# RWKV stage of a two-layer trunk: a list scheduler that also models the DMA queue and the staging buffers, and a norm over two row tiles

## The chip, the core and the metric

The kernel runs on one core of one Trainium2 chip. The metric is the device time of one execution in microseconds (us), as the median of three runs. The engines are named as the profile names them: PE is TensorE (PEld its weight loads), DVE is VectorE, ACT is ScalarE, POOL is GpSimd, and SP is SyncE, which here issues nearly all DMAs, in the order of its program. Each engine works through its own program in order; an instruction whose inputs are not there holds up everything behind it on that engine.

## What is computed

The input is 512 rows of 1024 channels. Layer 0 is an RWKV-7 time mixing, layer 1 a differential attention; each is followed by a layer norm over a scaled residual and a squared-ReLU MLP with another such norm. Everything is float32. Cut to what the change touches, layer 0 is

```
xx = token_shift(x) - x
r, k, v = (x + xx*mu[0]) @ w_r, (x + xx*mu[2]) @ w_k, (x + xx*mu[3]) @ w_v
w = -softplus(-(w0 + tanh(xw @ w1) @ w2)) - 0.5
a = sigmoid(a0 + (xa @ a1) @ a2);   g = sigmoid(xg @ g1) @ g2
kk = k*k_k / norm(k*k_k);   k = k * (1 + (a - 1) * k_a)
# per head of 64 channels, over the 512 rows:
S_t = S_{t-1} diag(exp(-exp(w_t))) + (S_{t-1} a_t) b_t^T + v_t k_t^T,  a_t = -kk, b_t = kk*a
y_t = S_t r_t
y = layer_norm(y per head) + sum(r*k*r_k) * v
h = (y * g) @ w_o
x = layer_norm(ALPHA*x + h)           # the norm that the change pairs
```

## The kernel before

Matrix products of the float32 data are made as three products of high and low parts (`mm3`, L138 to L143), so each weight is loaded, cast to a high part by ACT and subtracted to a low part by POOL or DVE.

The RWKV stage (`rwkv`, L172) works on eight pairs of heads (128 channels), p = 0 to 7, in four groups g of two pairs. The recurrence is cut in eight chunks of 64 rows. Its work consists of small generators, each a step with a letter and a number:

- `K`, `L`, `H`, `M`: the low-rank parts and the mixed inputs.
- `u0` to `u23`: a weight unit of `w_k`, `w_r`, `w_v` (L293): two loads of 256 KB into the staging tile `wst` (three buffers), two casts to `whi` on ACT (L307), two subtractions to `wlo` on POOL (L310). `p0` to `p11`: the projections, four of k, four of r, four of v, 48 matmuls each (L315). `E`: evictions, which store k, r and v to DRAM (L348). `D`, `N`: the norms of k.
- `F`, the front of a pair (`front`, L574): loads `wa`, k, r and the norms (L581 to L588), four matmuls (L593, L594), a chain over ACT, DVE (L602, L620 to L624) and POOL (L91), then the bonus: a matmul (L640), a load of v (L645), a product on DVE (L649), a store to `bD` (L652).
- `A` (`amat`, L654): 16 matmuls (L671), four masked evictions on DVE (L676), a store to `nbD` (L679). `B` (`tmat`, L683): transposes (L697).
- `I` (`inverse`, L704), one for a group of two pairs: a load of `nu` from `nbD` (L714), 15 steps of two small DVE operations each (L724, L726), a store to `gbD` (L727). `J` (`inverse2`, L730): a load of `dc` from `gbD` (L738), then the rest of the inverse in a chain of PE, DVE and ACT, whose first matmul is L752.
- `U`, `X`, `S`, `Y`, `Z`: the solve, the values, the scan over the chunks (L868 to L883), the head norm, and the finish (L915), which loads `g2` (L919) and `bl`, the stored bonus (L921). `P`: preparation of `w_o` (two staging buffers, loads L391, ACT L396, POOL L400); `P0` also loads x into `acc` (L384, two loads of 1 MB). `W`, `V`: the output projection of a group and its addition to `acc`.

What stands in which order on the engines is decided while the program is built, by `order` (L515): a list scheduler that takes, of all steps whose needs are met, the one that can start first by its own count of the engines' time, and of those within `SLACK` the one with the longest path behind it (`SPAN`, a planned length for each letter). A yield names an engine and a planned duration. A yield `"SP"` is a plain delay: SP is not counted as an engine, so a DMA is issued wherever the plan stands at that moment, and the staging buffers are not counted.

The last group, `W(3)`, and the layer norm of each 128-row tile (`ln`, L986) are written after the list and ordered by the framework's own scheduler. `ln` takes one row tile: two BN_STATS (L992), an aggregate, a reciprocal root in ten small DVE operations (`rsqrt`, L93 to L103), an affine half on DVE (L1002, L1003), a normalised half on ACT (L1008), transposes on PE (L1022), then splits. The MLP's first matmuls come behind the four tiles' transposes.

## Time and profile before

| what | us |
|---|---|
| median of the runs | 1543.22 (1542.98 to 1543.57) |
| the profiled execution | 1538.03 |
| its span, first to last instruction | 1536.1 |
| PE busy in the span | 1393.3 (91%) |
| DVE, ACT, POOL busy | 732.4, 589.7, 324.7 |

The profiled execution is 5.2 us shorter than the median. The share of busy time is over the whole span; the RWKV stage, with the norm behind it, is about its first 539 us, and the idle time of PE lies mostly there. In the rows below a timeline row gives start, length, engine, line, operation and tiles, and in brackets the idle time just ahead of it with what ended it. "SPq" is SP issuing a DMA. [...]

### The profile page before, as it was taken

The page shows a single profiled execution, that of the slowest core. Times are in us where ns is not written, and L with a number is a line of the kernel's source. Part 1 is how long each engine was busy: PE and PEld are TensorE (multiplying, and loading weights), DVE is VectorE, ACT ScalarE, POOL GpSimd, SP SyncE. Part 2 cuts the span into 40 slices and gives each one's busy share as a digit, 9 for nine tenths or more (in the row PEclk, how much of TensorE's full clock was granted, in tenths as well). Part 3 has the DMA queues.
Part 4 walks back from the last instruction along what each step waited for, and adds up shares of the span by engine and source line. Part 5 has one row for each costly group of instructions (what it writes and reads, how often), then busy time and mean ns, then how long its engine had stood idle before and what let it go on. Part 6 is the DMA issues. An engine that isn't in the chain of part 4 may idle for free.

```text
span 1536.1 us, 25128 instructions
## 1 busy us (share of the span) xinstructions
PE 1393.3 (91%) x10200; PEld 1148.3 (75%) x10200; DVE 732.4 (48%) x1558; ACT 589.7 (38%) x1091; POOL 324.7 (21%) x252
## 2 busy tenths in 40 slices
PE   8999939689995499999999989999988999999997
PEld 3677718467783398888888878888877988888886
DVE  6210465668747723333333553456667433333346
ACT  7422434355243332332313244566554513233220
POOL 5344420311013220010101044223232201010010
PEclk9999959789997699999999999999988999999999
DMA  4234534332304213232323035223212433233311
GB/s 162 90 122 144 159 79 112 108 100 84 96 27 153 68 55 111 84 108 90 102 96 96 28 102 159 74 79 110 63 62 77 138 96 96 96 96 97 96 42 55
DMA packets 81155, 146.31 MB, mean 95 GB/s; under 512 B 32224, under 2 KB 36992, under 8 KB 81040
## 3 DMA queue, kind: packets, MB, share of 16 engines
q1 hardware_dynamic: 81040, 144.71, 30.6%
q8 instruction: 80, 1.31, 0.4%
q14 instruction: 35, 0.29, 0.1%
HBM read 127.30 MB, written 13.19 MB: 91 GB/s over the span
## 4 chain that ended last, share of the span: by engine, by line
PE 75%; DVE 13%; issue 4%; DMA 3%; SPq 2%; ACT 2%; POOL 1%; DVEq 0%; POOLq 0%; ACTq 0%
PE a L141 11%; PE a L142 11%; PE a L143 10%; PE o L142 5%; PE s L143 5%; PE o L143 5%; PE s L142 5%; PE s L141 5%; PE o L141 5%; PE o L1204 1%; PE e L259 1%; DMA wst<-in_wo 1%; PE e L260 1%; DVE gtm L724 1%; DVE gu L726 1%
## 5 line engine op out<-in xcount | busy, mean ns | idle before, releaser
L106 ACT CAST whi<-wst 128x1024 fp32r<-128x1024 f32 x160 | 168.0, 1053 | 314.7 <-PE a L143 124.5
L107 DVE TENSOR_TENSOR wlo<-wst,whi 128x1024 fp32r<-128x1024 f32 x120 | 147.5, 1230 | 234.0 <-ACT whi L106 234.0
L91 POOL TENSOR_TENSOR r<-r 128x512 f32<-128x512 f32 x64 | 67.6, 1056 | 536.3 <-ACT hh L1063 534.7
L141 PE MATMUL a<-ba,whi 128*128 128x512 f32 (+1 forms) x400 | 147.9, 370 | 2.6 <-DVE qT L1152 2.2
L142 PE MATMUL a<-ba,whi 128*128 128x512 f32 (+1 forms) x400 | 146.3, 366 | 0.0
L143 PE MATMUL a<-ba,wlo 128*128 128x512 f32 (+1 forms) x400 | 146.2, 365 | 0.0
L107 POOL TENSOR_TENSOR wlo<-wst,whi 128x1024 fp32r<-128x1024 f32 x40 | 96.1, 2417 | 168.3 <-ACT whi L106 167.9
L1065 DVE TENSOR_TENSOR hl<-r,hh 128x512 fp32r<-128x512 f32 x64 | 44.3, 692 | 146.5 <-POOL r L91 146.5
L141 PEld LDWEIGHTS a<-ba,whi 128*128 128x128 f32 x400 | 76.0, 190 | 18.1 <-issue 3.7
L143 PEld LDWEIGHTS a<-ba,wlo 128*128 128x128 f32 x400 | 76.0, 190 | 12.0
L142 PEld LDWEIGHTS a<-ba,whi 128*128 128x128 f32 x400 | 76.1, 190 | 11.4
L141 PE MATMUL s<-ba,whi 128*128 128x512 f32 (+1 forms) x232 | 81.9, 353 | 0.0
L143 PE MATMUL s<-ba,wlo 128*128 128x512 f32 (+1 forms) x232 | 81.6, 352 | 0.0
L142 PE MATMUL s<-ba,whi 128*128 128x512 f32 (+1 forms) x232 | 81.3, 351 | 0.0
L310 POOL TENSOR_TENSOR wlo<-wst,whi 128x512 fp32r<-128x512 f32 x48 | 61.8, 1304 | 86.8 <-ACT whi L307 86.8
L142 PE MATMUL o<-ba,whi 128*128 128x512 f32 (+1 forms) x200 | 71.8, 359 | 3.6 <-DVE ba L107 3.6
L141 PE MATMUL o<-ba,whi 128*128 128x512 f32 (+1 forms) x200 | 71.8, 359 | 1.3 <-ACT ba L106 1.3
L143 PE MATMUL o<-ba,wlo 128*128 128x512 f32 (+1 forms) x200 | 71.6, 358 | 0.0
L141 PE MATMUL o<-whi,hh 128*128 128x512 f32 x176 | 68.7, 390 | 0.0
L142 PE MATMUL o<-wlo,hh 128*128 128x512 f32 x176 | 68.6, 390 | 0.0
L143 PE MATMUL o<-whi,hl 128*128 128x512 f32 x176 | 68.3, 390 | 0.0
L142 PE MATMUL a<-wlo,hh 128*128 128x512 f32 x168 | 65.4, 390 | 0.0
(287 smaller groups left out, 3316.4 us busy)
## 6 DMA issues: line engine op xcount, KB each, us to landing
wst<-in_m SPq DMA_DIRECT2D x128, 512.0 KB, 3.7
wst<-in_kv SPq DMA_DIRECT2D x16, 512.0 KB, 3.9
wst<-in_wk SPq DMA_DIRECT2D x16, 256.0 KB, 7.2
wst<-in_wr SPq DMA_DIRECT2D x16, 256.0 KB, 4.1
wst<-in_wv SPq DMA_DIRECT2D x16, 256.0 KB, 3.3
wst<-in_wo SPq DMA_DIRECT2D x16, 256.0 KB, 7.1
wst<-in_q SPq DMA_DIRECT2D x8, 512.0 KB
kT<-kT SPq DMA_DIRECT2D x16, 256.0 KB, 2.9
```

What stands on the lines that cost most here:

```text
L91: return eng.tensor_tensor(out=out, in0=in0, in1=in1, op=ALU.mult)
L106: self.nc.scalar.copy(out=hi, in_=src)
L107: (lo_eng or self.nc.vector).tensor_tensor(out=lo, in0=src, in1=hi, op=ALU.subtract)
L141: mm(ps, lh, rh, start=first, stop=False)
L142: mm(ps, lh, rl, start=False, stop=False)
L143: mm(ps, ll, rh, start=False, stop=last)
L259: PE.matmul(ps, lx[:, c, c0:c0 + P], x0(c), start=(c == 0), stop=False)
L260: PE.matmul(ps, ls[:, c, c0:c0 + P], xs(c), start=False, stop=(c == NK - 1))
L310: G.tensor_tensor(out=lo[:, b:b + 2], in0=ss[b // 2], in1=hi[:, b:b + 2], op=ALU.subtract)
L724: V.tensor_tensor(out=tmv, in0=GU[:, 0:m, s:s + 1].to_broadcast([P, m, n]), in1=NU[:, s:s + 1, s + 1:16].to_broadcast([P, m, n]), op=ALU.mult)
L726: V.tensor_tensor(out=gv, in0=gv, in1=tmv, op=ALU.add)
L1065: V.tensor_tensor(out=hl, in0=r, in1=hh, op=ALU.subtract)
```

## The change

- `order` gets an engine `Q`, the DMA queue, free from 8.0 on, which is occupied in turn by every yield `"Q"`; loads and stores now stand behind such yields. The plain delay `"SP"` remains for the time to landing.
- It also counts the staging buffers: `ws` (3, of the projection weights) and `wo` (2, of `w_o`). Units `u` and `P` are cut in halves, each with its own load, cast and subtraction.
- The steps `F`, `A`, `B` of all pairs and `I0`, `I1` get 250 added to their rank, so they are taken first where they can start at about the same time as another step.
- The front's second part loads v ahead of its bonus matmul. The loads of `g2` and `bl` become a step of their own, `T`, ahead of `Z`. `P3` no longer waits for `W2` but for `P2`. Several planned durations are altered.
- `ln` takes a list of row tiles; behind `W(3)` it is called twice with two tiles (`last`), with one reciprocal root of two columns. The other norms call it with one tile.

The core of the diff:

```diff
 SLACK = 0.3
+EARLY = 250
@@ unit
                 for b in range(0, h, 2):
+                    yield "Q", 1.6, 1, "ws"
                     ss.append(self.t(self.ws, "wst", [P, 2, WCOL]))
                     nc.sync.dma_start(...)
-                yield "SP", 4.5
-                yield "ACT", 1.24
+                yield "SP", 2.2
                 for b in range(0, h, 2):
+                    yield "ACT", 0.62
                     S.copy(out=hi[:, b:b + 2], in_=ss[b // 2])
-                yield "POOL", 2.7
                 for b in range(0, h, 2):
+                    yield "POOL", 1.3
                     G.tensor_tensor(out=lo[:, b:b + 2], ...)
+                    self.drop(1, "ws")
@@ W(3)
+            def last(w):
+                ...
+                next(w)
+                for b in range(0, NT, 2):
+                    for _ in range(4):
+                        next(w, None)
+                    for i in range(2 * b, 2 * b + 4):
+                        self.add_out(el["w3"][i], i // 2, i % 2, 1.0)
+                    self.ln(0, gb, (b, b + 1), False)
@@ needs
-                need["Z%d" % p] = ["Y%d" % g, "F%d" % p] + (old("Z", 1) if q else []) + (["W%d" % (g - 1)] if g else [])
+                need["T%d" % p] = ["o1", "F%d" % p] + old("Z", 1)
+                need["Z%d" % p] = ["Y%d" % g, "T%d" % p] + (["W%d" % (g - 1)] if g else [])
-                need["P%d" % g] += ["S4", "S5"] if g == 3 else []
+                if g == 3:
+                    need["P3"] = ["S4", "S5", "P2"]
@@ order
         free = self.free = dict.fromkeys(("PE", "DVE", "ACT", "POOL", "SP"), 0.0)
+        free["Q"] = 8.0
-        self.left = {"e": 4, "in": 5, "cs": 1}
+        self.left = {"e": 4, "in": 5, "cs": 1, "ws": 3, "wo": 2}
+        early = ["%s%d" % (t, p) for t in "FAB" for p in range(8)] + ["I0", "I1"]
                 rank[n] = SPAN[n[0]] + max([path(m) for m in after[n]], default=0.0)
+                rank[n] += EARLY * (n in early)
@@ ln
-    def ln(self, i, gb, tt, final):
+    def ln(self, i, gb, tts, final):
+        lp, V, n = self.lnp, self.nc.vector, len(tts)
+        mv = self.t(lp, "mv", [P, n, 2], bufs=2)
+        for u, tt in enumerate(tts):
+            st = self.t(lp, "st", [P, 2, 6], bufs=2)
+            for j in range(2):
+                V.bn_stats(out=st[:, j, :], in_=self.acc[tt][:, j * T:(j + 1) * T])
+            V.bn_aggr(out=mv[:, u], in_=st)
+        v = self.t(lp, "ve", [P, n], bufs=2)
+        V.tensor_scalar_add(v.unsqueeze(2), mv[:, :, 1:2], LN_EPS)
+        r = self.rsqrt(lp, "lr", v, [P, n])
+        for u, tt in enumerate(tts):
+            self.ln_one(i, gb, tt, final, mv[:, u], r[:, u:u + 1])
```

What the scheduler makes of it is seen in the order of the instructions at three places.

The first place is PE from the last projection matmul to the first matmul of `J0`, which is L752 before. L640 is the bonus of a front, L671 belongs to `A`, L697 to `B`, L593 to a front's start; of each run of like rows the first stands.

```order
L143 MATMUL a_1289<-ba_315,wlo_1246 128x512
L640 MATMUL e_1452<-in_1299,rkb_1449 128x512
L671 MATMUL e_1475<-ar_1371,bk_1372 128x128
...
L697 MATMUL e_1498<-cst_58,bk_1372 128x64
...
L593 MATMUL e_1520<-hwa_129,wa_1456 128x512
...
L593 MATMUL e_1574<-hwa_129,wa_1565 128x512
...
L640 MATMUL e_1621<-in_1460,rkb_1611 128x512
L671 MATMUL e_1641<-ar_1549,bk_1550 128x128
...
L697 MATMUL e_1676<-cst_58,bk_1550 128x64
...
L752 MATMUL e_1710<-ba_1670,bb_1334 64x64 x16
```

That is the bonus of pair 1, `A1`, `B1`, the starts of fronts 2 and 3, the bonus of pair 2, `A2`, `B2`, and then `J0`. The same stretch of the changed kernel, where L144 ends the projections, L688 is `A`, L715 `B`, L660 the bonus and L773 the first of `J0`:

```order
L144 MATMUL a_1613<-ba_313,wlo_1462 128x512
L688 MATMUL e_1706<-ar_1652,bk_1653 128x128
...
L715 MATMUL e_1734<-cst_58,bk_1653 128x64
...
L660 MATMUL e_1760<-in_1535,rkb_1701 128x512
L773 MATMUL e_1768<-ba_1719,bb_1027 64x64 x16
L777 MATMUL e_1788<-cst_58,ar_958 64x64 x16
```

Only `A3`, `B3` and the bonus of pair 3 are left there; everything listed before, and the starts of `A0` to `A2`, now stands among the projections of r and v.

The second place is SP at the start of `P0`, behind the `dc` loads of pairs 2 and 3. `acc` is x, `wst` from `in_wo` the staging of `w_o`, and `wa`, `in` from `kD`, `rD`, `rnD` the loads of front 5. Before:

```order
L738 DMA dc_2264<-gbD_71 64x8x16 x2
L384 DMA acc_2267<-in_x 128x2x1024
L384 DMA acc_2269<-in_x 128x2x1024
L391 DMA wst_2272<-in_wo 128x512
L391 DMA wst_2273<-in_wo 128x512
L391 DMA wst_2420<-in_wo 128x512
L391 DMA wst_2421<-in_wo 128x512
L581 DMA wa_2428<-in_wa 128x128
L583 DMA in_2430<-kD_64 128x512
L585 DMA in_2432<-rD_65 128x512
L588 DMA in_2434<-rnD_67 64x512 x2
```

The same place of the changed kernel:

```order
L759 DMA dc_2342<-gbD_71 64x8x16 x2
L392 DMA acc_2364<-in_x 128x2x1024
L596 DMA wa_2444<-in_wa 128x128
L598 DMA in_2446<-kD_64 128x512
L600 DMA in_2448<-rD_65 128x512
L603 DMA in_2450<-rnD_67 64x512 x2
L656 DMA in_2477<-vD_66 128x512
L392 DMA acc_2497<-in_x 128x2x1024
L668 DMA bD_69<-bs_2514 128x512
L401 DMA wst_2555<-in_wo 128x512
```

The loads of front 5 stood behind both loads of x and four of `w_o`; now they stand behind one load of x and ahead of all of `w_o`.

The third place is DVE at the first norm behind `W(3)`: additions to `acc` (L954), statistics, affine half (L1002, L1003) and the reciprocal root (`lr`). Before:

```order
L954 SCALAR_TENSOR_TENSOR acc_2267<-acc_2267,e_5330 128x512
L992 BN_STATS st_5346<-acc_2267 128x6
L954 SCALAR_TENSOR_TENSOR acc_2267<-acc_2267,e_5338 128x512
L992 BN_STATS st_5346<-acc_2267 128x6
L994 BN_AGGR mv_5349<-st_5346 128x2
L996 TENSOR_SCALAR ve_5351<-mv_5349 128x1
L1002 SCALAR_TENSOR_TENSOR acc_2267<-acc_2267,mv_5349,bc_5327 128x512
L97 TENSOR_SCALAR lr_5353<-ve_5351 128x1
L100 TENSOR_TENSOR lr_5354<-lr_5353 128x1
...
L1003 SCALAR_TENSOR_TENSOR acc_2267<-acc_2267,lr_5353,bc_5327 128x512
```

The changed kernel, where L981 adds, L1019 takes statistics and L1035 and L1036 are the affine half:

```order
L981 SCALAR_TENSOR_TENSOR acc_2364<-acc_2364,e_5351 128x512
L1019 BN_STATS st_5363<-acc_2364 128x6 x2
L1019 BN_STATS st_5367<-acc_2364 128x6 x2
L1020 BN_AGGR mv_5362<-st_5363 128x2
L1020 BN_AGGR mv_5362<-st_5367 128x2
L1035 SCALAR_TENSOR_TENSOR acc_2364<-acc_2364,mv_5362,bc_5327 128x512
L1022 TENSOR_SCALAR ve_5371<-mv_5362 128x2
L1035 SCALAR_TENSOR_TENSOR acc_2364<-acc_2364,mv_5362,bc_5327 128x512
L98 TENSOR_SCALAR lr_5373<-ve_5371 128x2
...
L108 TENSOR_TENSOR wlo_5597<-wst_5598,whi_5596 128x1024
L1036 SCALAR_TENSOR_TENSOR acc_2364<-acc_2364,lr_5373,bc_5327 128x512
```

Four additions (the last of them is shown) now come ahead of all four statistics, one reciprocal root serves two tiles, and a weight subtraction of the MLP stands ahead of the second affine step.

## Rows read from the trace of the kernel before

**Rows 1.** Windows: stretch, length, busy us (count) of PE, PEld, DVE, ACT, POOL, PEclk, DMA.
```profile
196.00:231.00 35.00, 12.74 (x73) 7.67 (x73) 24.83 (x54) 13.47 (x24) 8.27 (x6) 0.50 0.28 70
...
264.00:301.00 37.00, 23.43 (x413) 18.78 (x413) 21.53 (x49) 12.95 (x25) 12.95 (x10) 0.77 0.46 147
301.00:342.00 41.00, 33.53 (x748) 27.93 (x748) 27.88 (x89) 21.32 (x48) 2.33 (x2) 0.83 0.33 86
```

**Rows 2.** Timeline of PE, end of the projections to `J0`.
```profile
171.51 0.69 PE L593 MATMUL e<-hwa,wa 64*128 64x512 f32 x1 [0.46 <-DMA wa<-in_wa]
...
184.03 0.71 PE L697 MATMUL e<-cst,bk 64*128 64x64 f32 x16
...
187.11 0.39 PE L142 MATMUL a<-ba,whi 128*128 128x512 f32 x1
187.34 0.39 PE L143 MATMUL a<-ba,wlo 128*128 128x512 f32 x1
187.56 1.02 PE L640 MATMUL e<-in,rkb 128*128 128x512 f32 x2
188.51 2.06 PE L671 MATMUL e<-ar,bk 64*128 64x128 f32 x32
...
231.41 1.97 PE L752 MATMUL e<-ba,bb 64*64 64x64 f32 x32 [4.96 <-DVE ba L748]
```

**Rows 3.** Waits of PE from 160 to 232: line, releaser, us in total, times, longest.
```profile
PE e L671 <- DVE bs L649: 9.0, 1, 9.0
```

**Rows 4.** Timelines of PE and SP, the start of `P0` and front 5.
```profile
281.08 1.19 PE L593 MATMUL e<-hwa,wa 64*128 64x512 f32 x1 [10.18 <-DMA wa<-in_wa]
...
265.42 12.81 SPq L391 DMA_DIRECT2D wst<-in_wo  x4
278.29 0.42 SPq L581 DMA_DIRECT2D wa<-in_wa  x1
```

**Rows 5.** Timelines of DVE and POOL: `I0` first and last step, fronts' products.
```profile
206.74 1.23 DVE L724 TENSOR_TENSOR gtm<-gu,nu 128x15 f32<-128x15 f32 x1
...
214.79 0.18 DVE L726 TENSOR_TENSOR gu<-gu,gtm 128x15 f32<-128x15 f32 x1
...
180.59 1.62 POOL L91 TENSOR_TENSOR in<-in,in 128x512 f32<-128x512 f32 x1
...
206.34 1.59 POOL L91 TENSOR_TENSOR in<-in,in 128x512 f32<-128x512 f32 x1
```

**Rows 6.** Groups by form, POOL, 60 to 490: busy us, mean ns | idle before.
```profile
L310 POOL TENSOR_TENSOR wlo<-wst,whi 128x512 fp32r<-128x512 f32 x38 | 49.3, 1312 | 61.8 <-ACT whi L307 61.8
```

**Rows 7.** DMA issues on the page: line, count, KB each, median us to landing.
```profile
wst<-in_wk SPq DMA_DIRECT2D x16, 256.0 KB, 7.2
...
wst<-in_wv SPq DMA_DIRECT2D x16, 256.0 KB, 3.3
```

**Rows 8.** Timelines of SP, PE, POOL and DVE, the finish and the norm.
```profile
461.84 16.71 SPq L391 DMA_DIRECT2D wst<-in_wo  x3
...
481.28 2.04 PE L934 MATMUL e<-hg,g 128*128 128x512 f32 x2 [4.91 <-DMA g<-in_g]
...
488.27 9.71 POOL L107 TENSOR_TENSOR wlo<-wst,whi 128x1024 fp32r<-128x1024 f32 x4
488.62 0.69 DVE L992 BATCH_NORM_STATS2 st<-acc 128x6 f32<-128x512 f32 x1
...
493.58 2.12 DVE L100 TENSOR_TENSOR lr<-lr 128x1 f32<-128x1 f32 x1
498.04 0.16 DVE L102 SCALAR_TENSOR_TENSOR lr<-lr,lr 128x1 f32<-128x1 f32 x1
...
500.30 1.94 PE L1022 MATMUL e<-cst,acc 128*128 128x128 f32 x8 [10.83 <-DVE nm L1007]
514.51 2.03 PE L1022 MATMUL e<-cst,acc 128*128 128x128 f32 x8 [7.90 <-DVE acc L1003]
537.17 2.04 PE L1022 MATMUL e<-cst,acc 128*128 128x128 f32 x8 [5.60 <-DVE acc L1003]
```

More of the change, by code (lines that the diff above doesn't have):

```diff
@@ L388, in prep @@
                     w = big("bb" if g == 3 else "ba", [P, 2, D], F32R)
-                    ss = [self.t(self.cm2, "wst", [P, T], bufs=2) for _ in range(2)]
-                    for n in range(2):
-                        nc.sync.dma_start(out=ss[n], in_=a["wo"][2 * g + q][:, n * T:n * T + T])
-                    yield "SP", 3.5
-                    yield "ACT", 1.24
                     for n in range(2):
                         cs = slice(n * T, n * T + T)
-                        S.copy(out=w[:, 0, cs], in_=ss[n])
-                    yield "POOL", 2.7
-                    for n in range(2):
-                        cs = slice(n * T, n * T + T)
-                        G.tensor_tensor(out=w[:, 1, cs], in0=ss[n], in1=w[:, 0, cs], op=ALU.subtract)
+                        yield "Q", 1.6, 1, "wo"
+                        ss = self.t(self.cm2, "wst", [P, T], bufs=2)
+                        nc.sync.dma_start(out=ss, in_=a["wo"][2 * g + q][:, cs])
+                        yield "SP", 2.2
+                        yield "ACT", 0.62
+                        S.copy(out=w[:, 0, cs], in_=ss)
+                        yield "POOL", 1.3
+                        G.tensor_tensor(out=w[:, 1, cs], in0=ss, in1=w[:, 0, cs], op=ALU.subtract)
+                        self.drop(1, "wo")
                     wos[g].append(w)
@@ L420, in W @@
                         self.done("t%d" % (8 * g + 2 * tt + n))
-                        if g == 3:
-                            self.add_out(ps, tt, n, 1.0)
-                    if g == 3:
-                        self.ln(0, gb, tt, False)
+            def last(w):
+                self.xh, self.xl = ([self.t(rp, "ba", [P, 4, T], F32R, bufs=4) for _ in range(2)] for _ in range(2))
+                gb = big("bc", [P, 2, D])
+                gb = [gb[:, 0, :], gb[:, 1, :]]
+                self.ln_load(0, gb)
+                self.lnp, self.psT, self.tT = self.cm2, self.psE, "e"
+                next(w)
[5 more added lines that the diff above has]
+                    self.ln(0, gb, (b, b + 1), False)
             def add(g):
@@ L448, in rwkv @@
                     "J": group(self.inverse2), "U": group(self.solve), "X": group(self.values), "S": group(self.scan),
-                    "Y": lambda z: self.stats(z, el[2 * z], el[2 * z + 1]), "Z": group(self.finish),
+                    "Y": lambda z: self.stats(z, el[2 * z], el[2 * z + 1]), "Z": group(self.finish), "T": group(self.gate),
                     "P": prep, "W": W, "V": add}
@@ L493, in rwkv @@
             manual.close()
-            for _ in W(3):
-                pass
+            last(W(3))
         self.lnp = self.pool("ln", 1, side="right")
@@ L612, in front @@
         S.activation(out=cs, in_=cs, func=AF.Exp, scale=CDEC)
-        yield "DVE", 3.6
+        yield "DVE", 4.4
         def c3(t):
@@ L626, in front @@
         d.update(ar=ar, bk=bk, pc=pc)
-        yield "POOL", 3.7
+        yield "POOL", 4.1
         self.mul(G, ar[:, :, 0, :], c3(rnb), E1[:, :, 0:CH])
@@ L637, in front @@
         self.done("G%d" % p)
+        yield "wait", "D%d" % (8 + p // 2)
+        yield "Q", 0.35, 1, "in"
+        v32 = self.t(ep, "in", [P, T], bufs=5)
+        nc.sync.dma_start(out=v32, in_=self.vD[p])
+        yield "SP", 2.2
         yield "PE", 0.95, 1
@@ L641, in front @@
         self.drop(1, "in")
-        yield "wait", "D%d" % (8 + p // 2)
-        yield "SP", 0.0, 1, "in"
-        v32 = self.t(ep, "in", [P, T], bufs=5)
-        nc.sync.dma_start(out=v32, in_=self.vD[p])
-        yield "SP", 2.2
         yield "DVE", 0.7
@@ L677, in amat @@
             self.drop(2)
+        yield "Q", 0.7
         for h in range(2):
@@ L913, in stats, with gate @@
                 S.activation(out=yn[:, c], in_=py[:, c], func=AF.Identity, scale=rs[:, u:u + 1], bias=nm[:, u:u + 1])
+    def gate(self, p, d):
+        nc = self.nc
+        yield "Q", 0.7
+        d["g2"] = self.t(self.cm, "g2", [P, P], bufs=2)
+        nc.sync.dma_start(out=d["g2"], in_=self.a["g2"][:, p * P:(p + 1) * P])
+        d["bon"] = self.t(self.ep, "bl", [P, T])
+        nc.sync.dma_start(out=d["bon"], in_=self.bD[p])
+        yield "SP", 2.4
     def finish(self, p, d):
@@ L989, in ln @@
         x = self.acc[tt]
-        st = self.t(lp, "st", [P, 2, 6], bufs=2)
-        for j in range(2):
-            V.bn_stats(out=st[:, j, :], in_=x[:, j * T:(j + 1) * T])
-        mv = self.t(lp, "mv", [P, 2], bufs=2)
-        V.bn_aggr(out=mv, in_=st)
-        v = self.t(lp, "ve", [P, 1], bufs=2)
-        V.tensor_scalar_add(v, mv[:, 1:2], LN_EPS)
-        r = self.rsqrt(lp, "lr", v, [P, 1])
         g2, b2 = (z.rearrange("p (j t) -> p j t", j=2) for z in gb)
```

40 lines of the change are left out of this document (21 added, 19 removed).

## The prediction

> **What bounds the kernel now.** I read the granted clock and the busy shares by stage first, then PE's own timeline with its waits, then the queue of SP, then DVE and POOL where these waits lead. PE is the bound of the program as a whole, so time can be had only where PE stands still or runs at its lower clock. Behind about 540 us nothing is moved but single neighbours, and I count that at nothing: the dense matmuls there hide it, and a weight that came late would cost a wait of PE of a few us at most. Ahead of it there are three places.
>
> The first is the hole behind the projections. Their last matmul begins at 187.34 us and the inverse of pair 0 begins at 231.41 [rows 2]: 43.7 us. [...] The second is 264 to 342 us: PE is busy 23.4 of 37 us at 0.77 and 33.5 of 41 us at 0.83 [rows 1]; multiplied, some 18 and 28 us of work at full clock, so 19 and 13 us are lost. One wait is named there: PE stands 10.2 us for the load of `wa` of front 5, and SP issues that load at 278.29, behind four loads of `w_o` that took from 265.42 to 278.23 to issue, as their two staging buffers came free [rows 4]. The third is the end of the stage: PE waits 4.9 us for a gate weight, since SP was held by loads of `w_o` from 461.84 for 16.7 us, and then the norm of each row tile stops PE, for 10.8, 7.9, about 5.6 and 5.6 us [rows 8] (the third row tile is like the fourth).
>
> **Term 1, fronts and `I0` among the projections.** Nothing is added to PE; it is moved. Ahead of `J0` and behind the last projection stood a bonus (0.95 us from start to next start), `A1` (2.0), `B1` (0.7), the four matmuls of fronts 2 and 3 (twice 1.1), another bonus, `A2` and `B2` (one of each stands in [rows 2]): 9.6 us at the full clock. All of it now lies ahead of the end of the projections, which so moves from 187.7 to 197.3 if nothing starves. Behind it stand only `A3`, `B3` and a bonus, 3.8 us, and `J0`.
>
> What can starve? (a) On SP the store of `I0` now stands ahead of the loads of front 3, of the last weight of the projections, and of the stores of two bonuses and of `A2`; PE reads front 3's load between two quarters of a projection, so a late `I0` stops it. `I0` took 206.74 to 214.97, 8.2 us, with POOL nearly idle [rows 5]. (b) On DVE two bonuses and `A2` stand behind `I0`, and each holds a PSUM bank that PE's next step needs. (c) POOL works on weights: two subtractions of 1.31 us [rows 6] for every 24 matmuls, which at 0.23 us apart [rows 2] last 5.5 us, so 48% of the time. In the trace a DVE operation on two tiles in SBUF doesn't run beside POOL: the first step of `I0`, otherwise 0.2 us, took 1.23 and ended at 207.97, with POOL's product at 207.93 [rows 5]; in the norm an operation on a single column took 2.12 us while POOL worked and the like 0.16 when it had ended [rows 8]. Stretched by 1/(1 - 0.48), `I0` is 15.8 us, 7.6 longer. I take 4 us of PE's time for (a) to (c) together, between 0 and 9: the fronts' gaps on POOL cover part of it.
>
> [...]
>
> From the projections' end to `J0`: `A3` itself 2.06, its first masks and `J0`'s two operations on DVE, and before that the load of `dc`, which waits on SP for the last stores. I estimate 8 us, between 5 and 15; the front's chain ahead of `A3` is no longer than its cover (front 1: 171.51 to 182.21 on POOL [rows 2, 5], 10.7 us, against five quarters of a projection, 13.7 us). So `J0` begins at 197.3 + 4 + 8 = 209.3, 22.1 us earlier, and has 3.8 us of work behind it that it had ahead. Term 1 is -25 us, between -8 and -33.
>
> **Term 2, the middle.** The loads of front 5 now stand ahead of all of `w_o`, behind one load of x of 1 MB. I take the 10.2 us of that wait and 3 us of the lower clock that followed it, -13. It may reach -28, if most of the 32 lost us go; or +10, one wait of this size, if a new load takes that place: the two loads of x, the masks' stores and the `T` loads all pass through the same queue, and their order is planned with constants. DVE is busy 21.5 of 37 and 27.9 of 41 us there [rows 1], so it is no bound yet, but near one where PE speeds up.
>
> **Term 3, the finish and the norm.** `P3` no longer waits for `W2`, so its weights and the gate's load leave SP early: 3 of the 4.9 us (between 0 and 4.9; the last `bl` still waits for `Z6`). Four norms' stops of 10.8, 7.9, 5.6 and 5.6, together 29.9 us, become two. A single chain is 5.6 us undisturbed. The first pair has four additions and four statistics of 0.69 us [rows 8] where a single has one addition and one statistic behind its last matmul, one more affine step, and a weight's subtraction ahead of its second: I put it at 10.5 us, and at 12 with POOL's four subtractions (9.7 us [rows 8]), which now mostly run beside the additions and statistics. The second pair, whose banks come one by one, has one statistic and one affine step more: 7 us. So 29.9 - 19 + 3 = 13.9, term 3 is -14, between -5 and -20. The saved rows of the reciprocal root, ten of 0.16 us a pair, are in that.
>
> **Sum.** -25 - 13 - 14 = -52 us. The profiled execution's own time is 1538.0, so 1486; the median stood 5.2 us above it, so I forecast 1543.2 - 52 = 1491 us.
>
> **The rivals.** (A) `I0` behind POOL. If every step of `I0` waits for POOL as the first did, `I0` takes all of 15.8 us; the load of front 3, the masks and the evictions come later, PE stops 9 instead of 4 us, and `J0` follows 14 instead of 8 us behind the projections. 11 us are gone: 1502. [...] For it speaks the 1.23 us step, against it that POOL pauses between weights.
>
> (B) The middle gives it back. `J0` comes early, but the scan and the next fronts then meet new loads on SP: term 2 is +10 instead of -13, 1514. For it speaks that half of the losses from 264 to 342 have no named cause; against it that the one named is removed.
>
> (C) The order does not do what it says. SP's waits are set by engines, not by its own occupation, which is all that `Q` counts: if the waits move along with the work, terms 1 and 2 vanish and term 3 stays: 1529. Against it: on PE the work really stands elsewhere.
>
> (D) Slower: the weights of the projections starve. From `u10` on, 28 half units now share the queue with fronts. A half unit lasts PE 12 x 0.23 = 2.73 us; it occupies one of three staging buffers for its landing and 1.31 us on POOL (the cast on ACT left out). With a landing of 3.3 us [rows 7] that is 1.5 us a half unit, hidden. With 7.2 us, as for `w_k` [rows 7], it is 2.84, and 28 x 0.11 = 3 us are lost. From about 12.5 us of landing, SP's waits included, 28 x 1.87 = 52 us are lost and the change is not worth anything; at 14 us it is 66 and the time 1557. Against it: the landing would have to be four times that of `w_v`.
>
> **How the numbers follow.** Forecast 0.49, A 0.16, B 0.13, C 0.08, D 0.08, and 0.06 for better than 1472, term 2 at its end (1476) with a little more. The forecast's own range, from the bounds of the terms, is 1472 to 1508. The range that should hold 8 in 10 reaches to A and B and leaves C and D out: 1468 to 1520. A measurement of this kernel can tell about 0.2% from no change, 3 us. Faster by more: all but D and a remainder of C and B, 0.89; slower 0.08; within 0.2% 0.03.
>
> **What would show it.** In the profile of the changed kernel the first matmul of `J0` should begin between 202 and 218 us, and the clock in the stretch ahead of it should stay near 1.00; PE's wait for `wa` of front 5 should be under 3 us; ahead of the transposes of the norm there should be two stops of PE, 9 to 13 and 6 to 8 us; and no L141-like matmul of the projections should wait more than a few us for a weight. The steps are wrong if the steps of `I0` average well over 0.3 us, if SP stands at the store of `I0` or of a bonus while a weight is due, or if between 230 and 330 us a new wait of 10 us stands. The forecast is wrong as a whole if PE idles among the projections as long as it did behind them.

## The result, and the profile after

| | before | after |
|---|---|---|
| median of the runs, us | 1543.22 (1542.98 to 1543.57) | 1491.45 (1488.13 to 1494.75) |
| profiled execution, us | 1538.03 | 1488.13 |
| its span, us | 1536.1 | 1486.4 |
| first matmul of `J0` | 231.41 | 210.19 |
| last head norm on ACT (16 ACTIVATE of `Y3`) | 469.03 | 441.42 |
| subtraction for the last `yhl`, the end of the finish | 485.23 | 453.71 |
| first matmul of the MLP | 538.85 | 489.67 |
| from there to the end of the span | 997.2 | 996.7 |

The changed kernel takes 0.966 of the time of before, 95% interval 0.963 to 0.970: 51.8 us less by the medians, 49.7 by the two spans. One execution each of runs 3 and 8 below took 5930.7 and 1760.1 us, far longer than its fellows, and their medians leave it out. The marks in the table (starts) cut the spans in pieces, and nothing comes from behind the last of them. 21.2 us come ahead of `J0`, 6.4 between `J0` and the last head norm, 3.9 between that and the end of the finish, 17.6 between the finish and the MLP. `A3`, `B3` and a bonus, 3.8 us of work, moved from the second piece to the first. So the three terms are 25.0, 2.6 and 3.9 + 17.6 = 21.5 us.

The windows of the changed kernel, to be held against [rows 1] (start and end, length, then busy us and count of PE, PEld, DVE, ACT and POOL, then PEclk, the granted clock as a share of the full one, DMA share, GB/s):

```profile
187.00:210.00 23.00, 19.98 (x119) 15.04 (x117) 9.53 (x12) 9.94 (x18) 7.02 (x5) 1.00 0.38 110
...
264.00:301.00 37.00, 28.03 (x746) 23.93 (x742) 29.34 (x74) 26.43 (x57) 12.05 (x9) 0.99 0.44 122
301.00:342.00 41.00, 27.25 (x308) 20.13 (x303) 37.06 (x129) 12.08 (x30) 5.18 (x4) 0.89 0.26 62
...
454.00:490.00 36.00, 15.81 (x69) 13.25 (x69) 30.98 (x65) 17.88 (x29) 18.29 (x10) 0.72 0.51 166
```

Ahead of `J0` PE is now busy 20 of 23 us at a clock of 1.00, where before it was busy 12.7 of 35 at 0.50 [rows 1], its longest wait there 9.0 us for a bonus on DVE [rows 3]. From 264 to 301 the clock rose from 0.77 to 0.99. From 301 to 342 PE is busy *less* than before, 27.3 against 33.5 us, and DVE 37.1 of 41.

PE's timeline from the stop among the projections to `J0` (it answers to [rows 2]):

```profile
179.31 1.93 PE L660 MATMUL e<-in,rkb 128*128 128x512 f32 x2 [3.60 <-DVE bs L664]
182.37 0.36 PE L715 MATMUL e<-cst,bk 64*128 64x64 f32 x1 [1.12 <-DVE bs L664]
...
202.90 0.48 PE L688 MATMUL e<-ar,bk 64*128 64x128 f32 x2
...
210.19 1.97 PE L773 MATMUL e<-ba,bb 64*64 64x64 f32 x32 [2.31 <-DVE ba L769]
```

The projections end at 202.9, where `A3` (L688) begins, and `J0` (L773) comes 7.3 us later. Among the projections PE stops for the bonus (`bs`, L664): 3.6 us for the first, which stands behind `I0` on DVE, and 1.1 for the second, which waits 2.45 us for the store of the first, since `bs` has one buffer.

The new wait in the middle. PE's waits from 100 to 500 us (line, releaser, us in total, times, longest), then the timelines of PE and DVE around 332 us:

```profile
PE e L142 <- DVE acc L981: 11.3, 2, 10.2
...
332.04 0.39 PE L144 MATMUL e<-ba,yhl 128*128 128x512 f32 x1
342.62 0.80 PE L142 MATMUL e<-ba,yhl 128*128 128x512 f32 x1 [10.19 <-DVE acc L981]
...
334.83 0.13 DVE L743 TENSOR_TENSOR gtm<-gu,nu 128x15 f32<-128x15 f32 x1
341.79 0.18 DVE L745 TENSOR_TENSOR gu<-gu,gtm 128x15 f32<-128x15 f32 x1
341.88 2.47 DVE L981 SCALAR_TENSOR_TENSOR acc<-acc,e 128x512 f32<-128x512 f32 x4
```

`W0` has written its PSUM banks and must wait until `V0` (L981) has added the first to `acc`. On DVE `V0` stands behind all fifteen steps of `I3` (L743, L745). Before, `V0` (L954) stood ahead of `I3` (L724), as DVE's timeline of the kernel before has it:

```profile
372.12 5.03 DVE L954 SCALAR_TENSOR_TENSOR acc<-acc,e 128x512 f32<-128x512 f32 x8
...
389.50 1.01 DVE L724 TENSOR_TENSOR gtm<-gu,nu 128x15 f32<-128x15 f32 x1 [0.73 <-DMA nu<-nbD]
```

The end of the stage, PE's timeline (it answers to [rows 8]):

```profile
469.07 3.65 PE L1055 MATMUL e<-cst,acc 128*128 128x128 f32 x16 [12.30 <-DVE nm L1040]
...
486.28 3.74 PE L1055 MATMUL e<-cst,acc 128*128 128x128 f32 x16 [7.89 <-DVE acc L1036]
489.67 0.54 PE L142 MATMUL s<-ba,whi 128*128 128x256 f32 x1
```

Two stops ahead of the transposes, 12.3 and 7.9 us, stand where there were four, and the wait of 4.9 us for the gate weight is gone.

### The profile page after: what moved, and what is told of

It is laid out like the page before. It is cut to its first block, busy times and chain, and to the rows that moved or that the text cites. A ratio compares the mean times of both kernels' runs of the same rounds, so it can differ in the third digit from the quotient of the medians.

```text
span 1486.4 us, 25115 instructions
## 1 busy us (share of the span) xinstructions
PE 1377.7 (93%) x10200; PEld 1138.8 (77%) x10200; DVE 736.1 (50%) x1536; ACT 589.0 (40%) x1091; POOL 326.3 (22%) x252
## 4 chain that ended last, share of the span: by engine, by line
PE 79%; DVE 14%; DMA 2%; issue 2%; ACT 2%; SPq 1%; POOL 0%; DVEq 0%; ACTq 0%; POOLq 0%
PE a L142 12%; PE a L143 11%; PE a L144 11%; PE o L143 5%; PE o L144 5%; PE o L142 5%; PE s L144 5%; PE s L143 5%; PE s L142 5%; PE o L1237 1%; DVE gtm L743 1%; PE e L260 1%; DVE gu L745 1%; PE e L261 1%; PE s L1217 1%
## 5 line engine op out<-in xcount | busy, mean ns | idle before, releaser
L142 PE MATMUL a<-ba,whi 128*128 128x512 f32 (+1 forms) x400 | 149.6, 374 | 2.7 <-DVE qT L1185 2.2
L143 PE MATMUL a<-ba,whi 128*128 128x512 f32 (+1 forms) x400 | 147.8, 370 | 0.0
L144 PE MATMUL a<-ba,wlo 128*128 128x512 f32 (+1 forms) x400 | 147.5, 369 | 0.0
L142 PEld LDWEIGHTS a<-ba,whi 128*128 128x128 f32 x400 | 77.0, 193 | 17.9 <-issue 3.2
L144 PEld LDWEIGHTS a<-ba,wlo 128*128 128x128 f32 x400 | 77.0, 193 | 12.4
L144 PE MATMUL s<-ba,wlo 128*128 128x512 f32 (+1 forms) x232 | 80.9, 349 | 0.0
L144 PE MATMUL o<-ba,wlo 128*128 128x512 f32 (+1 forms) x200 | 71.6, 358 | 0.0
L144 PE MATMUL o<-whi,hl 128*128 128x512 f32 x176 | 68.2, 390 | 0.0
```

The costliest lines, as they stand in the source:

```text
L142: mm(ps, lh, rh, start=first, stop=False)
L143: mm(ps, lh, rl, start=False, stop=False)
L144: mm(ps, ll, rh, start=False, stop=last)
```

## The experiments

All of the runs below are single edits of the changed kernel, of the kernel before, or of the run named. The kernel before ran beside them again, at medians of 1540.1 to 1541.2. Single executions of one kernel lie up to some 10 us apart (1538.0 to 1547.8 for the kernel before), so differences of a few us are read from the marks, which tell where they arise. But the marks come from one execution each, and they differ too: run 1 is the changed kernel's program up to `W(3)`, and its last head norm stands 3.8 us later (445.2 against 441.4 us), with as many matmuls from `J0` on but a mean clock of 0.92 instead of 0.96. The profiled execution of the changed kernel is its fastest. So a difference of less than some 4 us between two runs' pieces shows nothing by itself. The pieces of each run, in us:

| run | median | `J0` | `J0` to head norm | to end of finish | to MLP |
|---|---|---|---|---|---|
| before | 1543.2 | 231.4 | 237.6 | 16.2 | 53.6 |
| changed | 1491.5 | 210.2 | 231.2 | 12.3 | 36.0 |
| 1 row tiles apart | 1506.9 | 211.3 | 233.9 | 12.3 | 50.4 |
| 2 pairs alone | 1529.4 | 230.2 | 238.2 | 16.7 | 42.8 |
| 3 no rank | 1519.2 | 221.6 | 247.7 | 13.3 | 35.5 |
| 4 rank alone | 1519.9 | 225.8 | 221.6 | 17.9 | 54.0 |
| 5 additions first | 1493.4 | 211.6 | 229.8 | 12.1 | 40.9 |
| 6 no buffer count | 1490.3 | 209.7 | 230.8 | 12.4 | 35.8 |
| 7 no queue | 1500.4 | 214.0 | 238.5 | 11.3 | 36.2 |
| 8 `I0` in PSUM | 1491.9 | 212.6 | 235.2 | 12.3 | 37.0 |
| 9 short `I3` | 1483.9 | 210.6 | 226.1 | 12.2 | 35.9 |
| 10 bonus in place | 1486.8 | 209.6 | 230.3 | 12.3 | 36.6 |
| 11 both, 8 and 10 | 1480.2 | 205.9 | 227.2 | 12.2 | 36.8 |
| 12 and an early `dc` | 1480.7 | 207.8 | 230.3 | 12.6 | 35.6 |

In 3 and 2, as before, the 3.8 us of `A3`, `B3` and a bonus stand behind `J0`; in the changed kernel, 1 and 4 they stand ahead.

### 1 and 2: what the pairing is worth

Run 1 changes `last` in the changed kernel:

```
-for b in range(0, NT, 2):
-    for _ in range(4):
+for b in range(NT):
+    for i in range(2 * b, 2 * b + 2):
         next(w, None)
-    for i in range(2 * b, 2 * b + 4):
         self.add_out(el["w3"][i], i // 2, i % 2, 1.0)
-    self.ln(0, gb, (b, b + 1), False)
+    self.ln(0, gb, (b,), False)
```

> Against the changed kernel (median 1491.4 us; its norm stops PE twice, 12.3 and 7.9 us). Here the list scheduler stays as changed, but the last output projection, its additions and its norm go one row tile at a time, as before the change. Theory (the pairing itself is worth what the four stops of before cost more than the two of after, 29.9 - 20.2 = 9.7 us): 9 to 15 us slower than the changed kernel, 1500 to 1506. Four stops stand ahead of the transposes again. Rival (the stage's end won through the early loads of w_o and of the gate alone, and the pairing only gathers the same waits): 1489 to 1495.

Run 2 puts `last` and the two-tile `ln` of the change into the kernel before, and nothing else.

> Against the kernel before (1543.2 us). Only the pairing of row tiles in the last projection and norm is added; the list scheduler stays as before. Theory (pairing is independent of the rest): 9 to 12 us faster, 1531 to 1534; the wait of 4.9 us for the gate weight stays. Rival (pairing pays only where the weights of the last group come early, as in the changed kernel): within 4 us of before.

Run 1 is 15.5 us slower than the changed kernel, just beyond the 9 to 15 expected, and 14.4 of them lie between the finish and the MLP. Run 2 is 11.8 us faster than before, 10.8 of them there. PE's stops ahead of the transposes in run 1:

```profile
468.41 1.94 PE L1054 MATMUL e<-cst,acc 128*128 128x128 f32 x8 [9.23 <-DVE nm L1039]
483.99 2.03 PE L1054 MATMUL e<-cst,acc 128*128 128x128 f32 x8 [9.05 <-DVE acc L1035]
495.29 2.03 PE L1054 MATMUL e<-cst,acc 128*128 128x128 f32 x8 [5.63 <-DVE acc L1035]
506.19 2.03 PE L1054 MATMUL e<-cst,acc 128*128 128x128 f32 x8 [5.70 <-DVE acc L1035]
```

They add up to 29.6 us, against 20.2 in the changed kernel: 9.4 of the 14.4. The windows of this stage in the kernel before, in run 1 and, above, in the changed kernel:

```profile
486.00:539.00 53.00, 22.34 (x75) 16.37 (x75) 37.77 (x87) 20.48 (x32) 21.30 (x12) 0.65 0.32 105
```
```profile
458.00:508.00 50.00, 20.38 (x75) 15.73 (x73) 36.45 (x88) 19.68 (x31) 19.31 (x10) 0.73 0.33 113
```

PE is busy 22.3, 20.4 and 15.8 us in them, and 9.4 + 4.6 = 14.0 accounts for run 1. Of the 4.6 us some 1.4 are six matmuls that the paired order runs ahead of the mark (69 instructions in place of 75; PE is busy 10.9 instead of 9.5 us in the finish). The other 3.2 I put down to the clock. The mean of the stretch, 0.73 and 0.72, doesn't show it, but the matmuls behind the stops do. Behind the first stop of run 1 the first eight gaps from start to start are about 0.43 us, as in the kernel before from 502.0 to 504.5 us, at a granted clock of 0.50; in the changed kernel, from the third matmul behind the transposes on, they are 0.23, at 1.00 from 474 to 478. One of each, from the timelines of run 1 and of the changed kernel:

```profile
471.00 0.63 PE L144 MATMUL e<-bb,yhl 128*128 128x512 f32 x1
```
```profile
473.44 0.40 PE L142 MATMUL e<-bb,yhl 128*128 128x512 f32 x1
```

With half as many stops less of the same work runs at the lower clock. The other 53.6 - 50.4 = 3.2 us of this piece are there without the pairing. That the early weights bring them is likely (0.8 us of PE's waits for `bb`, L400, are gone), but not shown. The gate's wait lies ahead of it: the finish is 3.9 us shorter in the changed kernel and in run 1, and not in run 2.

In run 2 the MLP's first matmul waited 3.9 us more than in the changed kernel:

```profile
527.86 0.58 PE L141 MATMUL s<-ba,whi 128*128 128x256 f32 x1 [3.87 <-DVE ba L107]
```

With that taken off, run 2 says 14.7 us for the pairing, as run 1 does. Both rivals fall. Why this matmul waits in runs 2 and 5 for the last of four splits and in the changed kernel only for the first is open: in run 5 DVE and POOL have the splits behind the norm in the same order.

### 3 and 4: rank and queue, each alone

Run 3, in the changed kernel:

```
-EARLY = 250
+EARLY = 0
```

> Against the changed kernel (1491.4 us). Only the 250 added to the rank of fronts, their matrices and the first two inverses is 0; queue, staging buffers and pairing stay. Theory (the rank is what puts the fronts and the first inverse among the projections, the queue's model only sets the order of loads): the inverse of pair 0 begins some 15 to 22 us later than 210 us, and the time is 1506 to 1513. Rival (counting queue and staging is what moves them, since weights then can't run ahead and the fronts' steps are startable first): inverse of pair 0 within 5 us of 210, time 1488 to 1496.

Run 4 adds only the rank (`EARLY`, and its line in `path`) to the kernel before.

> Against the kernel before (1543.2 us). Only the 250 on the rank of fronts, their matrices and the first two inverses is added, to the old scheduler which counts neither queue nor staging buffers. Theory (rank alone carries the first term, about -21 us at the inverse of pair 0, and the middle stays as it was): 1518 to 1526, inverse of pair 0 at 208 to 216 us. Rival (without the queue's model the early fronts stand in front of weights that are late, and projections starve): 1540 to 1560, with PE waits for weights among the projections.

Neither alone does it, and both theories missed: run 3 is slower than its 1506 to 1513 us, with `J0` only 11.4 us later, and run 4 is in time within its range but has `J0` at 225.8 instead of 208 to 216. Ahead of `J0` the rest of the change without the rank wins 9.8 us, and the rank alone 5.6 + 3.8 = 9.4; together they win 25.0, 5.8 more than the sum. What the rank lacks in run 4 stands in the timelines of PE and SP:

```profile
181.49 1.19 PE L596 MATMUL e<-hwa,wa 64*128 64x512 f32 x1 [8.29 <-DMA wa<-in_wa]
...
167.53 6.80 SPq L303 DMA_DIRECT2D wst<-in_wv  x2
...
179.08 0.42 SPq L584 DMA_DIRECT2D wa<-in_wa  x1
```

SP stands 6.8 us at two weight loads, loads of v and a bonus's store follow, and `wa` of the next front, which PE is already due to read, is issued at 179.08. It is a late load of a front, not of a weight as in the prediction's rival D, and the rest of the change takes it away.

In the middle the two pull against each other. From `J0` to the last head norm the rank alone wins 16.0 - 3.8 = 12.2 us, and the rest of the change alone *loses* 10.1, though PE's wait for `wa` of front 5 is gone in either run. In run 3 PE waits there 8.8 us for the additions of L981, as it waits 10.2 in the changed kernel. In run 4 that wait is 1.4. It doesn't hang on `I3` alone: in run 3 `V0` begins at 347.78, far ahead of `I3` (396.63), and PE waits all the same; in run 4 `V0` stands right behind `I3` (DVE's timeline, then PE's), and the wait is short, with matmuls of `J` (L766, L778, L786) among those of `W0` on PE:

```profile
359.48 0.18 DVE L729 TENSOR_TENSOR gu<-gu,gtm 128x15 f32<-128x15 f32 x1
359.58 4.86 DVE L957 SCALAR_TENSOR_TENSOR acc<-acc,e 128x512 f32<-128x512 f32 x8
...
360.31 0.50 PE L142 MATMUL e<-ba,yhl 128*128 128x512 f32 x1 [1.41 <-DVE acc L957]
```

So where `W0` stands on PE counts as well. No run moved that alone.

### 5 and 9: what the new wait is worth

Run 5, in `order` of the changed kernel:

```
-best.append((at, -path(n), n))
+best.append((at, -path(n) - 1000 * (n[0] == "V"), n))
```

> Against the changed kernel (1491.4 us). One edit: among steps that can start at about the same time, the additions of an output projection to the residual are taken first (1000 on their own rank, none on what precedes them). So the eight additions of group 0 stand among the statistics of the head norm instead of behind all fifteen steps of the inverse of group 3. Theory (PE's new wait of 10.2 us at 332 us is the order on DVE: the output projection has filled its six banks and waits for the additions): that wait falls below 3 us, and the time is 4 to 9 us shorter, 1482 to 1487. Rival (DVE itself is the bound there, 37.1 of 41 us busy: the wait goes to the inverse of group 3 and the steps behind it): the wait is shorter, but another of like size stands on PE between 320 and 380 us, time 1488 to 1495.

Run 9, in its `inverse`:

```
             yield "DVE", 0.48
+            if g == 3 and s < 13:
+                continue
```

> Against the changed kernel (1491.4 us). The inverse of group 3 does only the last two of its fifteen steps, so that part of the result of group 3 is left out; the plan and every other instruction stay in their order. It takes 26 DVE operations, 6.1 us of DVE, out from between the head norm of group 1 and the additions of group 0, at 335 to 341 us. Theory (DVE is the bound from 301 to 360 us, so what one of its chains gains the other loses; only less work on DVE helps): PE's wait of 10.2 us is about 6 us shorter, and here, unlike in the run that only moved the additions, the last cast of the finish comes 4 to 7 us earlier, time 1484 to 1488. Rival (behind 342 us another chain sets the pace, PE or the scan): the wait shrinks and the last cast moves by less than 2 us, 1489 to 1493.

In run 5 the wait of 10.2 us is gone and no PE wait over 3.0 us stands between 320 and 380 us in its place, but the time is not shorter: my theory's time failed, and so did the rival's wait. The first matmul of `J6`, in the timelines of PE in the changed kernel, in run 5 and in run 9, tells where it went:

```profile
378.37 1.15 PE L773 MATMUL e<-ba,bb 64*64 64x64 f32 x32
```
```profile
374.06 1.15 PE L773 MATMUL e<-ba,bb 64*64 64x64 f32 x32
```
```profile
374.19 1.15 PE L775 MATMUL e<-ba,bb 64*64 64x64 f32 x32
```

PE has the same work ahead of it in all three. Counted from `J0`, run 5 reaches `J6` 5.7 us earlier than the changed kernel and run 9 4.6. Run 9, where everything behind stands in its old order, keeps 5.1 us to the last head norm, and is 7.6 us faster in all by the medians, 5.4 by the spans. The changed kernel and runs 1, 6 and 8 have one order on DVE, ACT and POOL in the middle and took 230.8 to 235.2 us for it, so that run 9's 226.1 is 5 to 9 us less. Run 5 gives 4.3 back between `J6` and the head norm: its edit moved the additions of groups 1 and 2 too, so that PE's order behind `J6` is another. A further 4.9 go at the MLP's first matmul, which waits as in run 2:

```profile
PE s L142 <- DVE ba L108: 3.9, 1, 3.9
```

In run 5 `I3` ends at 358.08 instead of 341.79 us, and `J6` still begins earlier. So `I3` had that slack, and in the changed kernel the order "`V0` behind `I3`" cost PE some 5 us or somewhat more, less than the wait's 10.2. Run 9 came out within its theory's numbers, but "DVE is the bound there", the reason given, does not hold, since run 5 brings `J6` as early with all of DVE's work in place: DVE is at 90% because a chain that nobody was waiting for stood ahead of one that PE was waiting for.

### 6 and 7: buffers or queue

Run 6, in `order` of the changed kernel:

```
-self.left = {"e": 4, "in": 5, "cs": 1, "ws": 3, "wo": 2}
+self.left = {"e": 4, "in": 5, "cs": 1, "ws": 99, "wo": 99}
```

> Against the changed kernel (1491.4 us). The plan counts no staging buffers (their numbers in the plan are set so high that they never bind; the buffers themselves stay three and two); the queue, the rank and the pairing stay. Theory (what carries the end of the projections is that each load has its time on the queue; the buffers' count adds little): 1489 to 1496, inverse of pair 0 within 4 us of 210. Rival (the count is what holds loads of w_o and of projection weights back from standing at SP while their buffer is full): PE waits for a load of wa or for a weight return, 1498 to 1512.

Run 7 keeps the count and lets every yield on `Q` pass at once.

> Against the changed kernel (1491.4 us). A yield on the queue takes no time and no turn in the plan; staging buffers, rank, halves and pairing stay. Theory (the queue's times are what puts the loads of the fronts ahead of other loads in time): the wait for wa of 8 us among the projections that the rank alone has is back, 1500 to 1512, inverse of pair 0 at 214 to 226 us. Rival (halves and staging count are enough): 1488 to 1497. One of this and the run without the staging count should be as slow as rank and pairing alone (1543.2 - 21.3 - 11.8, some 1510).

The count of the staging buffers adds nothing: run 6 is within 1 us of the changed kernel at every mark. The queue's times are worth 9 us: without them `J0` is 3.8 us later, the middle 7.3 longer, and a wait of 5.3 us for `wa` is back. Run 7 is still some 10 us better than rank and pairing alone (1510 by their sum). It has the units and `P` cut in halves, the gate's load as a step of its own, `P3` behind `P2` and other planned durations; which of them it is was not tried. In the middle it is the other way round: 238.5 us against 221.6 with the rank alone, so that these other parts cost some 17 us there, and the queue's times win 7.3 of them back.

### 8, 10, 11 and 12: `I0` among the projections

Run 8, in `inverse` of the changed kernel, ahead of the steps; `NP` and the product `tm` of group 0 are parts of the bank `bk`, and the steps read `NP` in place of `NU`:

```
+        if g == 0:
+            yield "ACT", 0.4, 1
+            bk = self.bank()
+            NP = bk[:, 0:256].rearrange("p (s t) -> p s t", t=16)
+            nc.scalar.copy(out=NP, in_=NU)
```

> Against the changed kernel (1491.4 us). The first inverse keeps its triangle and its product in a PSUM bank (one copy by ACT more), so that none of its DVE steps reads two tiles in SBUF; the second operand of each is in PSUM. Its 30 steps took 13.1 us of their own, eight of them 1.17 to 1.33 us long while POOL worked. Theory (DVE with two SBUF inputs is blocked for as long as a POOL operation runs): no step over 0.6 us while POOL works, the inverse's steps 6 to 9 us together, and the inverse of pair 0 0 to 5 us earlier; time 1487 to 1492. Rival (the long steps wait for something else, as POOL's shared traffic or their inputs): steps over 1 us stay, 1490 to 1496, since one bank less is left to the fronts.

First the changed kernel's `I0`, timelines of DVE and POOL, then the same steps in run 8:

```profile
166.19 1.20 DVE L743 TENSOR_TENSOR gtm<-gu,nu 128x39 f32<-128x39 f32 x1
167.43 1.33 DVE L745 TENSOR_TENSOR gu<-gu,gtm 128x39 f32<-128x39 f32 x1
168.79 1.22 DVE L743 TENSOR_TENSOR gtm<-gu,nu 128x48 f32<-128x48 f32 x1
170.04 1.21 DVE L745 TENSOR_TENSOR gu<-gu,gtm 128x48 f32<-128x48 f32 x1
171.29 0.22 DVE L743 TENSOR_TENSOR gtm<-gu,nu 128x55 f32<-128x55 f32 x1
...
164.08 3.25 POOL L92 TENSOR_TENSOR ar<-in,e 128x512 f32<-128x512 f32 x2
167.41 1.30 POOL L92 TENSOR_TENSOR in<-in,in 128x512 f32<-128x512 f32 x1
168.66 2.53 POOL L312 TENSOR_TENSOR wlo<-wst,whi 128x512 fp32r<-128x512 f32 x2
```
```profile
167.94 0.23 DVE L749 TENSOR_TENSOR e<-gu,e 128x63 f32<-128x63 f32 x1
169.96 0.20 DVE L749 TENSOR_TENSOR e<-gu,e 128x39 f32<-128x39 f32 x1
...
167.71 1.30 POOL L92 TENSOR_TENSOR in<-in,in 128x512 f32<-128x512 f32 x1
168.97 2.54 POOL L312 TENSOR_TENSOR wlo<-wst,whi 128x512 fp32r<-128x512 f32 x2
```

With both operands in SBUF a step of 0.2 us ends with the POOL operation beside it (six of the 30 took 1.17 to 1.33 us, not eight); with one in PSUM no step of the 30 took over 0.23 us, and 28 of them took 6.7 us together. The rival falls. The inverse of pair 0 did not follow: it began at 212.6, 2.4 us later. The last two operations of `I0` were planned behind two bonuses, of which the first waited 2.4 us for PE and the second 3.9 for the store from `bs`, so `I0` ended at 178.9, as late as in the changed kernel (178.6); the bonus behind it waited another 4.7 us for `bs`.

Run 10 writes the bonus over v, stores it from there, and gives the room of `bs` to a sixth `in`. Run 11 is both.

```
-        bon = self.t(ep, "bs", [P, T])
-        V.tensor_tensor(out=bon, in0=pb, in1=v32, op=ALU.mult)
+        V.tensor_tensor(out=v32, in0=pb, in1=v32, op=ALU.mult)
```

> Against the changed kernel (1491.4 us). The bonus is written over v in its own buffer, from which it is stored, instead of into the one buffer bs; the place of bs becomes a sixth buffer of that kind, and the plan counts six and holds each until its store has landed. Theory (the stop of PE of 5.6 us among the projections is the one buffer: the second and third bonus on DVE wait 2.45 and 1.10 us for the store of the one before, and PE waits 3.6 us for their bank): no such wait, the last projection ends 3 to 5 us earlier, and so does the inverse of pair 0 (205 to 208 us): time 1485 to 1489. Rival (the bonuses are late anyway, since they stand behind the first inverse on DVE): inverse of pair 0 within 2 us of 210, 1489 to 1494.

> The run before this, with the first inverse in a PSUM bank as well, whose 28 steps so took 6.7 us beside POOL instead of 13.1. In the run that had this alone the last two operations stood behind two bonuses, each of which waited for the store of the one before, and 7.7 us of the gain were lost there. Theory: without that buffer both gains add up, inverse of pair 0 at 202 to 207 us, 1483 to 1488. Rival (the end of the projections is set by weights and PE alone, so the inverse's time is hidden): within 2 us of the run with the bonus in place alone.

In run 10 PE's wait for a bonus there is 0.6 us, but the end of the projections stays (`A3` begins at 203.31) and `J0` is at 209.6: the rival was right at this place. PE now waits 3.6 us ahead of a `B` (L714) for masks on DVE, which stand behind an `I0` that still has steps of 1.2 and 1.3 us. With `I0` in PSUM as well the projections end at 198.5 and `J0` comes at 205.9; the time is 1480.2 us, better than its theory's 1483 to 1488, ratio to before 0.960 (0.957 to 0.963). For `J0` both had to go. This version beats both kernels, the changed one by 11 us by the medians and 8.5 by the spans. Of these 4.3 lie ahead of `J0` and 4.0 in the middle.

The middle of runs 10 and 11 has another order than the changed kernel's, with one addition of `V0` ahead of `I3`: PE waits at most 1.8 us for additions there, and none of its other stops reaches 2.6. That buys little: 230.3 us in run 10, 227.2 in run 11. In run 10 PE idles 24.6 us there, 9.9 less than in the changed kernel, but its 4262 matmuls take 205.7 us at a mean clock of 0.92 where they took 196.7 at 0.96. Whether the lower clock belongs to the order or to the execution is open; run 1, with the changed kernel's program there, also has 0.92.

Run 12 starts from run 11 and takes the load of `dc` out of the second half of the inverse into a step of its own, which is planned as soon as the inverse is stored.

> The run with the bonus in place and the first inverse in PSUM (1480.2 us, inverse of pair 0 at 205.9, projections ended at 198.2), with one edit more: the load of dc is a step of its own, planned as soon as its inverse is stored, instead of the first act of the second half of the inverse behind the end of the projections, where its four pieces for two pairs took SP 4.25 us to issue from 199.62 and held the first DVE step until 204.33. Theory (of the 8 us between the projections and the inverse of pair 0 most is this load): inverse of pair 0 at 200 to 203 us, time 1475 to 1478. Rival (DVE is as late, since masks of pair 3 and steps of the inverse of group 1 now stand ahead there, or SP stands at this load among the projections and a weight is late): inverse of pair 0 within 2 us of 206, time 1479 to 1484.

The timelines of SP, DVE and PE in run 11, then of DVE and PE in run 12:

```profile
199.62 4.25 SPq L766 DMA_DIRECT2D dc<-gbD  x4
...
204.33 0.69 DVE L774 TENSOR_TENSOR tt<-dc,cst 128x512 f32<-128x512 f32 x1 [2.17 <-DMA dc<-gbD]
...
205.92 1.97 PE L780 MATMUL e<-ba,bb 64*64 64x64 f32 x32 [4.89 <-DVE ba L776]
```
```profile
201.94 0.17 DVE L749 TENSOR_TENSOR gtm<-gu,nu 128x15 f32<-128x15 f32 x1 [6.28 <-DMA nu<-nbD]
...
206.20 0.69 DVE L780 TENSOR_TENSOR tt<-dc,cst 128x512 f32<-128x512 f32 x1
...
207.76 1.97 PE L786 MATMUL e<-ba,bb 64*64 64x64 f32 x32 [3.98 <-DVE ba L782]
```

The load came early, and the rival was right: with the fronts done sooner, eighteen operations of `I1`, which has the high rank, stand ahead of `J0` on DVE from 201.94 on. The time stays that of run 11. The 4.25 us that SP stood at the four loads in run 11 were not the issuing alone, either: in run 12 they are issued in two pairs of 1.70 and 1.35 us, and in the kernel before the same four took 2.96.

## Why the prediction was right, point by point

The forecast was 1491 us and the median is 1491.45. The direction and the three places were right, and one term was right in size. The fit of the total is luck in part: term 2 fell 10 us short and term 3 came out 7.5 larger. The range of 1472 to 1508 is also narrower than the bounds of the terms that it is said to come from: added up, they reach from 1462 to 1540. And the 43.7 us of the hole count from the end of the last projection matmul, not from its start as written.

**Term 1, -25 forecast, -25.0 measured.** Most steps hold too. The projections were put at 197.3 + 4 and ended at 202.9, 5.6 us late (bounds 0 to 9), of which PE's waits are 4.9; 8 us on to `J0` were estimated and are 7.3; `J0` was put at 209.3 and came at 210.2. `I0` did stretch as feared: 13.1 us of its own (15.8 at worst, 8.2 undisturbed). Its 30 steps average 0.41 us, so the prediction's own sign that the steps are wrong, well over 0.3, appeared, though the size came out as allowed for. Of the candidates for the stop, what stands behind `I0` on DVE, bonus and masks, and the one buffer of the bonus were the ones: with both mended (run 11) the projections end 4.4 us earlier, with either alone (runs 8 and 10) they don't. The load of front 3 was not. Rival A, by which the blocking would go through to `J0` in full, was wrong in size: run 11 against run 10 puts the whole effect of the blocking of `I0` at 3.7 us of `J0`. Rival D did not come about: no matmul of the projections is seen to wait for a weight, in the changed kernel or in run 4, where what is late is `wa` of the fronts.

**Term 2, -13 forecast, -2.6 measured.** This is the step that failed. The wait for `wa` of front 5 went, as forecast, and the clock up to 301 us came back; run 4, with -12.2, comes to the size forecast, by the rank alone. But the rest of the change costs 10 us there, alone (run 3) and on top of the rank (231.2 against 221.6), and I had put the whole gain of the middle down to its order of the loads. It isn't the queue's times that cost, since without them the middle is 7.3 us longer (run 7). I named loads as the only thing that could take the place of the removed wait. What took it was no load but additions on DVE for which PE waits 10.2 us, in the changed kernel behind `I3`. Runs 5 and 9 put that at some 5 us or somewhat more. The prediction's own sign for it, a new wait of 10 us between 230 and 330 us, appeared 2 us behind that stretch. Why the rest of the change brings that wait with or without `I3` ahead (run 3), and where the remainder of the 10 us goes, stays open. PE's stops of 3.4, 3.0 and 2.5 us there in the changed kernel (L954 for ACT, L688 and L660 for masks on DVE) aren't the answer: run 10 has none of them, nor the 10.2, and its middle is 0.9 us shorter.

**Term 3, -14 forecast, -21.5 measured.** The wait for the gate was put at 3 and gave 3.9. The norm was put at 29.9 - 19 = 10.9 and gave 17.6. By its two stops it should have given less, since they took 12.3 and 7.9 us, above 12 and 7. The mis-sized term is what the sum left out: PE's own work between the stops, 22.3 us before and 15.8 after, since six matmuls run earlier (1.4 us) and less of the rest at a clock of 0.50. 9.7 + 6.5 make 16.2 of the 17.6. I had counted the clock in term 2 and forgotten it here.

**Rivals B and C** did not come about: the middle gave most of its gain back, but not all and more (B needed +10), and the fronts moved in time as they did in the order.

## What to carry to other kernels

When a plan's costs change, look not only at the steps that the change names but at every pair of chains on a nearly full engine that changed places: ask which of the two someone is waiting for. A share of 90% on an engine (DVE, 37.1 of 41 us) is no proof that it is the bound. Taking work out (run 9) doesn't tell it, since that helps either way; a run that only moves the chain which nobody waits for out of the way (run 5) does. And the length of a stop of PE isn't what its removal brings: in the norm it brought more, 9.4 us of stops and 3.2 of lower clock behind them, and in the middle less, 5 to 9 us for a stop of 10.2 in run 9 and nothing in the time of run 5.

## What the runs showed of the hardware

In run 8 the second operand, moved from SBUF to PSUM, freed the small DVE operations of `I0` from POOL: the longest of the 30 took 0.23 us, where in the changed kernel six took 1.17 to 1.33. An operation with a single source of two columns was held as well, in the norm of the changed kernel, timelines of DVE and POOL, and the same form when POOL had long ended:

```profile
463.05 2.31 DVE L98 TENSOR_SCALAR lr<-ve 128x2 int32<-128x2 int32 x1
483.52 0.16 DVE L98 TENSOR_SCALAR lr<-ve 128x2 int32<-128x2 int32 x1
...
462.49 2.84 POOL L108 TENSOR_TENSOR wlo<-wst,whi 128x1024 fp32r<-128x1024 f32 x1 [0.65 <-ACT whi L107]
```

The 2.31 us end with the POOL operation. I had looked for this only at operations with two inputs; why this one is held, no run here tells.
